# Sums, diagonals and spreads of norm factors in separate steps, and the order of the last scalings, in a one-core streaming-encoder block

## The chip, the cores and the metric

The kernel runs on 1 core of one Trainium2 chip. A core has five engines with queues of their own, which run side by side and meet at semaphores: TensorE (PE in the profile, with its weight loads as PEld), VectorE (DVE), ScalarE (ACT), GpSimd (POOL) and SyncE (SP), which here issues the DMAs. The metric is the device time of one execution in microseconds, the median of several.

## The reference, cut to what matters

One layer of a streaming encoder on 256 tokens of 2048 features, all float32:

```
x = x + 0.5 * swiglu(rms_norm(x, ffn1_norm), w_gate, w_up, w_down)
h = rms_norm(x, mix_norm);  proj = h @ w_in        # pool | q | k | v | g | a
y_pool = pool_mixer(u);  y_gla = gla_mixer(q, k, v, g, a)
x = x + concat(y_pool, y_gla) @ w_out
x = x + mem_cross_attention(rms_norm(x), rms_norm(mem))
x = x + 0.5 * swiglu(rms_norm(x, ffn2_norm), ...)
out = rms_norm(x, final_norm)
```

Two norms matter here. In `gla_mixer` each of 4 heads has 256 features per token, and after the attention of a head its output is normalised per token and head and then gated:

```
o = o * lax.rsqrt(jnp.mean(o * o, axis=-1, keepdims=True) + RMS_EPS)
o = o * head_norm;  return o * silu(g)
```

The other is the last `rms_norm`, over the 2048 features of each token, the end of the kernel.

## The kernel before, in words

**Precision and weights.** Each weight matrix is streamed once from memory in units of 1 MB (`raw`, three buffers). ACT casts a unit to its rounded half (`wh`, line 210), DVE subtracts to get the rest (`wl`, line 211); both have three buffers, so the cast of unit u+3 waits until TensorE has let go of unit u. Every product is made of several matmuls with these halves: in `block_a`, whose output has features on the partitions (lines 239 to 269), a unit is 32 matmuls (line 261) into two accumulators `pa`; in `block_b` (tokens on the partitions) and `block_t` a unit is 48 matmuls (line 276).

**The stream.** `Stream` (lines 34 to 77) records weight units and side steps. `st.op(f, n)` places step `f` behind the n-th unit from where it is recorded; all engines' work is issued from that one list. Then the framework's scheduler reorders within each engine's queue by its own estimates, so a queue's order is that of the built program and not only of the list. Each engine executes its queue strictly in order, and an instruction that waits holds all behind it.

**PSUM.** All matmul results go to one pool of four buffers (`ptile`, line 104), two of which a `block_a` holds during its units.

**The GLA part** (lines 670 to 763). `block_b` for the values `v` runs twice (b = 0, 1), with four units each. For the two heads of each b, `scores(h)` builds scaled queries `QD` on DVE (line 693), makes four products into `pq` (line 701) and copies them to `ST` (line 707); `attend(h)` makes the head's output `po` from `ST` and `v` (lines 714, 717), squares it on ACT into `osq` (line 723, tile `t`) and copies it to `oz` (line 725, tile `m`). `head_norms(b)` then handles the two heads of b at once, in one step:

1. `token_sums` (line 187): DVE adds the two halves of the squares (line 189), and TensorE sums over the partitions by a product with a column of ones (line 191, tile `pn`).
2. `rsqrt` (line 175): DVE and ACT compute the four factor columns `r` (lines 178 to 185; the square root on ACT).
3. `spread` (line 195): DVE makes a diagonal matrix from each factor column (line 198, two buffers), and TensorE spreads it over all partitions by a product with ones (line 199, tile `ps`).
4. DVE multiplies `oz` by the result (line 739).

After both b there are two `block_a` for the output gate g, four units each, whose evictions `ev_g` (lines 741 to 753) join the two halves of `pa` (ACT copies one half at line 234, DVE adds at line 235) and use the scaled `oz`. `head_norms(0)` and `scores`/`attend` of heads 2 and 3 thus stand between the units of the first gate block, and `head_norms(1)` between the two gate blocks.

`finish_norm` (line 222) does the same spreading for the norms before `w_in` and before `w_q`: the spread rows `R` are copied out at line 230.

**The end** (`down_end`, lines 900 to 979). The last product w_down is ordered so that the 128 tokens of the first half (h = 0) get their last unit for all four column blocks (nb 0 to 3) first, and then the second half (h = 1). Each finished block is added to X by DVE (line 934), squared with a row sum by ACT (line 937), and multiplied with the gain by POOL (line 939; not the very last block). `row_factor` (line 941) makes the row factor of a half, and `finish` (line 945) scales a block, on ACT (line 953) where it is told so or else on DVE (line 955; line 949 for the very last one), and sends it out (line 956). `second_half` (line 958) orders these: factor and four scalings of half 0, around the last products of half 1, then factor and scalings of half 1.

Of the kernel before, what the change touches and what calls it, by code (L numbers as in the profile page):

```python
# [7 lines left out]
F32 = mybir.dt.float32  # L8
F32R = mybir.dt.float32r
AF = mybir.ActivationFunctionType  # L10
ALU = mybir.AluOpType
# [3 lines left out]
P = 128  # L15
D = 2048
S = 256
# [62 lines left out]
def build(ctx, tc, I, out):  # L80
    nc = tc.nc
    st = Stream()
# [21 lines left out]
    def ptile(name):  # L104
        return psum.tile([P, 2, NB], F32, tag="ps", name=name)
# [6 lines left out]
    def uid(s):  # L112
        cnt[0] += 1
        return f"{s}{cnt[0]}"
# [60 lines left out]
    def rsqrt(dst, sums, n, w):  # L175

        v, r = chain[:, 0, :w], chain[:, 1, :w]
        nc.vector.tensor_scalar(
            out=v, in0=sums, scalar1=0.25 / n, scalar2=0.25 * EPS, op0=ALU.mult, op1=ALU.add
        )  # L180
        nc.scalar.activation(r, v, AF.Sqrt)
        nc.vector.reciprocal(out=dst, in_=r)
        nc.vector.tensor_tensor(out=v, in0=v, in1=dst, op=ALU.mult)
        nc.vector.tensor_tensor(out=v, in0=v, in1=r, op=ALU.add)
        nc.vector.reciprocal(out=dst, in_=v)

    def token_sums(out, sq):

        nc.vector.tensor_tensor(out=sq[:, 0, :], in0=sq[:, 0, :], in1=sq[:, 1, :], op=ALU.add)
        for t in range(2):  # L190
            nc.tensor.matmul(
                out[:, t : t + 1], sq[:, 0, t * P : (t + 1) * P], ones[:, 0:1], start=True, stop=True
            )

    def spread(ps, col, t):

        d = tmp.tile([P, P], F32, tag="diag", name=uid("diag"), bufs=2)
        nc.vector.tensor_scalar_mul(d, ident, col)
        nc.tensor.matmul(ps[:, t * P : (t + 1) * P], ones, d, start=True, stop=True)  # L199

    def split_scaled(dst, kt, src, scale):
# [14 lines left out]
    def row_squares(src, c):  # L216

        for h in range(2):
            j = tmp.tile([P, S], F32, tag="j", name=uid("j"), bufs=2)
            nc.scalar.activation(j, src[h], AF.Square, accum_out=ss[:, h, c : c + 1])  # L220

    def finish_norm(n, spread_too=True):

        nc.vector.tensor_reduce(out=sums, in_=ss[:, :, :n], axis=AX.X, op=ALU.add)
        rsqrt(Rcol, sums, D, 2)
        if spread_too:
            ps = ptile(uid("ps"))
            for t in range(2):
                spread(ps[:, 0, :], Rcol[:, t : t + 1], t)
            nc.vector.tensor_copy(R, ps[:, 0, :S])  # L230

    def joined(ps, dst, scale=None):
        c = ctile()
# [94 lines left out]
    def wblock(w, n0, k0=0, nk=KT):  # L328

        def src(k):  # L330
            return lambda raw: wload(raw.rearrange("p (k n) -> p k n", n=NB), w, k, 4, n0)
        return [src(k0 + k) for k in range(0, nk, 4)]
# [107 lines left out]
    def into_x(w, act, scale, gain=None, k0=0, nk=KT, spread_too=True):  # L440

        for b in range(2):
            block_t(wwide(w, b * 2 * NB, k0, nk), act, residual(scale, b))
            if gain is not None:
                for j in range(2):
                    st.op(lambda c=2 * b + j: fold(c, gain), 1)
        if gain is not None:
            st.op(lambda: finish_norm(4, spread_too), 2)

    FF_PARTS = ((0, 4), (4, 4), (8, 3))  # L450

# [58 lines left out]
    mix = {}  # L510
# [198 lines left out]
    def attend(h):  # L709
        s, v = mix["ST"], mix["v"]  # L710
        po = ptile(uid("po"))
        for vt in range(2):
            col = h * DV + vt * P
            nc.tensor.matmul(
                po[:, vt, :S], v[:, 0, col : col + P], s[:, 0, :], start=True, stop=False
            )
            nc.tensor.matmul(
                po[:, vt, 2 * CH : S], v[:, 1, col : col + P], s[:, 1, 2 * CH :], start=False, stop=True
            )
        if h % 2 == 0:  # L720
            mix["oz", h // 2] = as_four(m4())
        q = mix["osq", h] = ttile()
        nc.scalar.activation(q, po[:, :, :S], AF.Square)
        i = h % 2
        nc.vector.tensor_copy(mix["oz", h // 2][:, 2 * i : 2 * i + 2, :], po[:, :, :S])

    def head_norms(b):
        pn = ptile(uid("pn"))
        for i in range(2):
            token_sums(pn[:, 0, 2 * i : 2 * i + 2], mix["osq", 2 * b + i])  # L730
        r = mt("r", [P, 4])
        rsqrt(r, pn[:, 0, :4], DV, 4)
        ps = ptile(uid("ps"))
        for i in range(2):
            for t in range(2):
                spread(ps[:, i, :], r[:, 2 * i + t : 2 * i + t + 1], t)
        for i in range(2):
            oz = mix["oz", b][:, 2 * i : 2 * i + 2, :]
            nc.vector.tensor_tensor(out=oz, in0=oz, in1=bc(ps[:, i, :S]), op=ALU.mult)
# [15 lines left out]
    for b in range(2):  # L755
        block_b(wblock(w_in, (4 + b) * NB), xs, ev_v(b))
        for i in range(2):
            h = 2 * b + i
            st.op(lambda h=h: scores(h), 1 + i)
            st.op(lambda h=h: attend(h), 2 + i)  # L760
        st.op(lambda b=b: head_norms(b), 4)
    block_a(wblock(w_in, 6 * NB), xs, ev_g(0))
    block_a(wblock(w_in, 7 * NB), xs, ev_g(1))
    st.op(close_scope, 1)
# [135 lines left out]
    def down_end(wd, k0, nk):  # L900

        acc_ps, kept = {}, []

        def mm(b, k, h, wh, wl):

            wh, wl = (w.rearrange("p (k j n) -> p k j n", j=2, n=NB) for w in (wh, wl))
            for j in range(2):
                nb = 2 * b + j
                if nb not in acc_ps:
                    acc_ps[nb] = ptile(uid("pe"))  # L910
                for kk in range(2):
                    products(acc_ps[nb][:, h, :], ys, k + kk, h, wh[:, kk, j], wl[:, kk, j],
                             k + kk == 0, k + kk == nk - 1)
                if k == nk - 2:
                    end_evict(nb, h)

        def unit(b, k):
            def fn(wh, wl):
                for h in range(2):
                    mm(b, k, h, wh, wl)  # L920
            return fn

        def end_unit(b):
            def fn(wh, wl):
                kept.append((wh, wl))
                mm(b, nk - 2, 0, wh, wl)
            return fn

        def end_evict(nb, h):
            cols = slice(nb * NB, (nb + 1) * NB)  # L930
            if h == 0:
                fin[nb] = scope["pool"].tile([P, 2, NB], F32, tag="sg", name=uid("O"), bufs=4)
            xn, o = X[:, h, cols], fin[nb][:, h, :]
            nc.vector.scalar_tensor_tensor(
                out=xn, in0=acc_ps[nb][:, h, :], scalar=0.5, in1=xn, op0=ALU.mult, op1=ALU.add
            )
            nc.scalar.activation(o, xn, AF.Square, accum_out=ss[:, h, nb : nb + 1])
            if nb < 3 or h == 0:
                nc.gpsimd.tensor_tensor(out=o, in0=xn, in1=fin["gB"][:, cols], op=ALU.mult)

        def row_factor(h):
            nc.vector.tensor_reduce(out=sums[:, h : h + 1], in_=ss[:, h, :4], axis=AX.X, op=ALU.add)
            rsqrt(Rcol[:, h : h + 1], sums[:, h : h + 1], D, 1)

        def finish(h, c, engine=None):
            cols = slice(c * NB, (c + 1) * NB)
            x, o, r = fin[c][:, h, :], X[:, h, cols], Rcol[:, h : h + 1]
            if h == 1 and c == 3:
                nc.vector.scalar_tensor_tensor(
                    out=o, in0=o, scalar=r, in1=fin["gB"][:, cols], op0=ALU.mult, op1=ALU.mult  # L950
                )
            elif engine is nc.scalar:
                nc.scalar.activation(o, x, AF.Copy, scale=r)
            else:
                nc.vector.tensor_scalar_mul(o, x, r)
            nc.sync.dma_start(out[0, h * P : (h + 1) * P, cols], o)

        def second_half():
            row_factor(0)
            finish(0, 0, nc.scalar)  # L960
            finish(0, 3)
            for b in range(2):
                mm(b, nk - 2, 1, *kept[b])
            finish(0, 1)
            finish(0, 2)
            row_factor(1)
            for c in range(4):
                finish(1, c, nc.scalar if c == 1 else None)

        def ready_sqrt():  # L970
            tc.keep_in_program_order(nc.scalar.activation(sums, Rcol, AF.Sqrt))

        st.op(ready_sqrt, 8)
        for b in range(2):
            for i, src in enumerate(wwide(wd, b * 2 * NB, k0, nk - 2)):
                st.unit(src, unit(b, 2 * i))
        for b in range(2):
            st.unit(wwide(wd, b * 2 * NB, k0 + nk - 2, 2)[0], end_unit(b))
        st.op(second_half)
# [66 lines left out]
```

## Time and profile before

| | |
|---|---|
| median of 3 runs | 2189.62 us (2189.52 to 2190.53) |
| the profiled execution, whole | 2187.98 us |
| its span in the trace | 2186.0 us |
| TensorE busy | 2152.8 us, 98% of the span |
| VectorE, ScalarE, GpSimd busy | 1116.3, 918.3, 14.3 us |
| mean DMA rate | 185 GB/s |

The span is what the trace covers, the first to the last instruction or transfer; the whole execution is 1.98 us longer. "Busy" of an engine says nothing about whether it sets the end; for that the trace can be asked what an engine waited for, and when. A row of the timeline gives the start and the duration in microseconds, the engine, the line of the kernel, the operation, the tile written and the tiles read, the shape and how many instructions (or records) are in the row; in square brackets stands how long the engine was idle before and who released it. "PEclk" is TensorE's granted clock as a share of full speed.

### The profile page before, as it was taken

How to read it: one execution, taken by the hardware profiler on the slowest of the kernel's cores; microseconds unless marked ns; L12 is line 12 of the kernel's file. 1: busy time of each engine (PE TensorE's matmuls, PEld its weight loads, DVE VectorE, ACT ScalarE, POOL GpSimd, SP SyncE). 2: the span in 40 equal slices, each digit the busy share in tenths (PEclk: the TensorE clock that was granted, in tenths of full speed). 3: DMA queues.
4: the chain of work that ended last, by engine and by line, in shares of the span. 5: the costliest groups of instructions: out<-in, count | busy, mean ns of one | idle time of the engine just before them, and what ended most of it. 6: DMA issues, size and time to landing. Idle time of an engine off the chain costs nothing.

```text
span 2186.0 us, 23828 instructions
## 1 busy us (share of the span) xinstructions
PE 2152.8 (98%) x10194; PEld 1803.2 (82%) x10194; DVE 1116.3 (51%) x850; ACT 918.3 (42%) x811; POOL 14.3 (1%) x41
## 2 busy tenths in 40 slices
PE   9999999999999999889999999999999999999997
PEld 7888888888888888778888888888888888888886
DVE  5544444455455576555656554554554444444544
ACT  6333333333334554345445443444433334333333
POOL 0000000000000000000000000000000000000001
PEclk9999999999999999999999999999999999999999
DMA  7555555555555555446555455655555555555553
GB/s 274 194 189 192 193 188 190 194 182 193 194 187 193 174 176 175 134 140 224 175 192 173 155 171 177 191 184 194 181 193 192 192 193 192 185 195 195 195 176 114
DMA packets 134674, 404.45 MB, mean 185 GB/s; under 512 B 8868, under 2 KB 12040, under 8 KB 134184
## 3 DMA queue, kind: packets, MB, share of 16 engines
q1 hardware_dynamic: 134536, 402.92, 55.3%
q8 instruction: 80, 1.31, 0.2%
q14 instruction: 26, 0.21, 0.0%
q10 hardware_dynamic: 32, 0.01, 0.0%
HBM read 400.80 MB, written 2.10 MB: 184 GB/s over the span
## 4 chain that ended last, share of the span: by engine, by line
PE 98%; DVE 1%; ACT 0%; issue 0%; DMA 0%; SPq 0%; DVEq 0%; ACTq 0%
PE pt L276 71%; PE pa L261 15%; PE pb L276 6%; PE pe L276 3%; PE ph L473 1%; PE pl L831 1%; PE pv L866 1%; PE px L428 0%; ACT wh L210 0%; PE ps L199 0%; DMA X<-in_x 0%; PE px L394 0%; PE pa L592 0%; PE tm L793 0%; PE pq L701 0%
## 5 line engine op out<-in xcount | busy, mean ns | idle before, releaser
L211 DVE TENSOR_TENSOR wl<-raw,wh 128x2048 fp32r<-128x2048 f32 (+2 forms) x382 | 865.0, 2264 | 976.1 <-ACT wh L210 976.0
L210 ACT CAST wh<-raw 128x2048 fp32r<-128x2048 f32 (+2 forms) x383 | 722.0, 1885 | 1093.6 <-PE pt L276 887.3
L276 PE MATMUL pt<-wh,xs 128*128 128x512 f32 x2816 | 871.8, 390 | 0.0
L276 PEld LDWEIGHTS pt<-wh,xs 128*128 128x128 f32 x2816 | 528.9, 188 | 109.4
L276 PE MATMUL pt<-wl,xs 128*128 128x512 f32 x1408 | 548.2, 389 | 0.0
L276 PE MATMUL pt<-wh,ys 128*128 128x512 f32 x1728 | 535.1, 389 | 0.0
L276 PEld LDWEIGHTS pt<-wh,ys 128*128 128x128 f32 x1728 | 324.4, 188 | 67.0
L276 PE MATMUL pt<-wl,ys 128*128 128x512 f32 x864 | 336.3, 389 | 0.0
L261 PE MATMUL pa<-xs,wh 128*128 128x512 f32 x896 | 321.2, 402 | 0.0
L276 PEld LDWEIGHTS pt<-wl,xs 128*128 128x128 f32 x1408 | 264.6, 188 | 54.7
L261 PE MATMUL pa<-xs,wl 128*128 128x256 f32 x896 | 250.0, 282 | 0.0
L261 PEld LDWEIGHTS pa<-xs,wh 128*128 128x128 f32 x896 | 169.4, 190 | 40.2 <-issue 0.5
L276 PEld LDWEIGHTS pt<-wl,ys 128*128 128x128 f32 x864 | 162.2, 188 | 33.5
L261 PEld LDWEIGHTS pa<-xs,wl 128*128 128x128 f32 x896 | 170.6, 190 | 1.3
L276 PE MATMUL pb<-wh,xs 128*128 128x512 f32 x384 | 121.9, 392 | 0.5 <-DVE ys L203 0.5
L276 PEld LDWEIGHTS pb<-wh,xs 128*128 128x128 f32 x384 | 72.0, 188 | 15.8 <-DVE ys L203 0.7
L276 PE MATMUL pb<-wl,xs 128*128 128x512 f32 x192 | 74.9, 390 | 0.0
L276 PE MATMUL pe<-wh,ys 128*128 128x512 f32 x192 | 59.4, 390 | 0.0
L276 PEld LDWEIGHTS pe<-wh,ys 128*128 128x128 f32 x192 | 36.0, 188 | 7.5
L276 PEld LDWEIGHTS pb<-wl,xs 128*128 128x128 f32 x192 | 36.1, 188 | 7.2
L276 PE MATMUL pe<-wl,ys 128*128 128x512 f32 x96 | 37.5, 390 | 0.0
L458 ACT ACTIVATE sg<-pt,Rcol 128x512 f32<-128x512 f32 x44 | 27.9, 686 | 21.6 <-PE pt L276 21.5
(164 smaller groups left out, 694.7 us busy)
## 6 DMA issues: line engine op xcount, KB each, us to landing
raw<-in_ffn_w_down SPq DMA_DIRECT2D x88, 1024.0 KB, 5.1
raw<-in_ffn_w_up SPq DMA_DIRECT2D x80, 1024.0 KB, 4.9
raw<-in_ffn_w_gate SPq DMA_DIRECT2D x77, 1024.0 KB, 5.0
raw<-in_w_in SPq DMA_DIRECT2D x32, 1024.0 KB, 5.1
raw<-in_xattn_w_kv SPq DMA_DIRECT2D x32, 1024.0 KB, 5.2
raw<-in_w_out SPq DMA_DIRECT2D x16, 1024.0 KB, 5.3
raw<-in_xattn_w_q SPq DMA_DIRECT2D x16, 1024.0 KB, 5.0
raw<-in_xattn_w_o SPq DMA_DIRECT2D x16, 1024.0 KB, 5.2
```

The lines of the kernel that those rows point to most:

```text
L210: nc.scalar.copy(hi, src)
L211: nc.vector.tensor_tensor(out=lo, in0=src, in1=f32(hi), op=ALU.subtract)
L261: nc.tensor.matmul(o, w, x, start=k == 0 and i == 0, stop=last and i == 1)
L276: nc.tensor.matmul(ps, a, w, start=first and i == 0, stop=last and i == 2)
L458: nc.scalar.activation(g[:, h, :], ps[:, h, :], AF.Silu, scale=Rcol[:, h : h + 1])
L473: nc.tensor.transpose(v[:, i, h * P : (h + 1) * P], g[:, h, i * P : (i + 1) * P], ident)
L831: nc.tensor.matmul(ps[:, t, :M], ys[:, 4 * h + d, a, tok], xa["K"][:, d, b, :], start=i == 0, stop=i == 11,)
L866: nc.tensor.matmul(ps[:, d, :S], xa["V"][:, m, a, col], xa["PT"][:, m, b, :], start=i == 0, stop=i == 5,)
```

## The change

`head_norms` loses its first and last parts. The DVE additions of the squares become `head_squares(h)`, a step of its own behind `attend(h)`. `head_norms(b)` keeps the sums over the partitions and the factors, and now makes all four diagonals at once (four buffers in place of two). The spreading products and the scaling of `oz` become `head_scale(b)`, one unit later. In the same way `finish_norm` keeps the factors and the diagonals, and `spread_norm` has the spreading products and the copy to `R`; `finish_norm` is placed one unit earlier than before and `spread_norm` where the whole was. In `rsqrt` the two small DVE operations become one with two scalar operands where there is a single column, which is so in `row_factor` alone. In `second_half` the scaling of block 1 of half 0 moves from DVE to ACT, and it and that of block 2 are recorded between the last products of column blocks 0, 1 and those of 2, 3.

```diff
         nc.scalar.activation(r, v, AF.Sqrt)
         nc.vector.reciprocal(out=dst, in_=r)
-        nc.vector.tensor_tensor(out=v, in0=v, in1=dst, op=ALU.mult)
-        nc.vector.tensor_tensor(out=v, in0=v, in1=r, op=ALU.add)
+        if w == 1:
+            nc.vector.tensor_scalar(
+                out=v, in0=v, scalar1=dst, scalar2=r, op0=ALU.mult, op1=ALU.add
+            )
+        else:
+            nc.vector.tensor_tensor(out=v, in0=v, in1=dst, op=ALU.mult)
+            nc.vector.tensor_tensor(out=v, in0=v, in1=r, op=ALU.add)
         nc.vector.reciprocal(out=dst, in_=v)
 
-    def token_sums(out, sq):
-
-        nc.vector.tensor_tensor(out=sq[:, 0, :], in0=sq[:, 0, :], in1=sq[:, 1, :], op=ALU.add)
-        for t in range(2):
-            nc.tensor.matmul(
-                out[:, t : t + 1], sq[:, 0, t * P : (t + 1) * P], ones[:, 0:1], start=True, stop=True
-            )
-
-    def spread(ps, col, t):
-
-        d = tmp.tile([P, P], F32, tag="diag", name=uid("diag"), bufs=2)
+    def diagonal(col):
+        d = tmp.tile([P, P], F32, tag="diag", name=uid("diag"), bufs=4)
         nc.vector.tensor_scalar_mul(d, ident, col)
+        return d
+
+    def spread(ps, t, d):
+
         nc.tensor.matmul(ps[:, t * P : (t + 1) * P], ones, d, start=True, stop=True)
...
         if spread_too:
-            ps = ptile(uid("ps"))
-            for t in range(2):
-                spread(ps[:, 0, :], Rcol[:, t : t + 1], t)
-            nc.vector.tensor_copy(R, ps[:, 0, :S])
+            diag["R"] = [diagonal(Rcol[:, t : t + 1]) for t in range(2)]
+
+    def spread_norm():
+
+        ps = ptile(uid("ps"))
+        for t in range(2):
+            spread(ps[:, 0, :], t, diag["R"][t])
+        nc.vector.tensor_copy(R, ps[:, 0, :S])
...
         if gain is not None:
-            st.op(lambda: finish_norm(4, spread_too), 2)
+            st.op(lambda: finish_norm(4, spread_too), 1)
+            if spread_too:
+                st.op(spread_norm, 2)
...
+    def head_squares(h):
+        sq = mix["osq", h]
+        nc.vector.tensor_tensor(out=sq[:, 0, :], in0=sq[:, 0, :], in1=sq[:, 1, :], op=ALU.add)
+
     def head_norms(b):
         pn = ptile(uid("pn"))
         for i in range(2):
-            token_sums(pn[:, 0, 2 * i : 2 * i + 2], mix["osq", 2 * b + i])
+            sq = mix["osq", 2 * b + i]
+            for t in range(2):
+                nc.tensor.matmul(
+                    pn[:, 0, 2 * i + t : 2 * i + t + 1], sq[:, 0, t * P : (t + 1) * P],
+                    ones[:, 0:1], start=True, stop=True,
+                )
         r = mt("r", [P, 4])
         rsqrt(r, pn[:, 0, :4], DV, 4)
+        mix["diag"] = [diagonal(r[:, i : i + 1]) for i in range(4)]
+
+    def head_scale(b):
         ps = ptile(uid("ps"))
-        for i in range(2):
-            for t in range(2):
-                spread(ps[:, i, :], r[:, 2 * i + t : 2 * i + t + 1], t)
+        for i in range(4):
+            spread(ps[:, i // 2, :], i % 2, mix["diag"][i])
         for i in range(2):
             oz = mix["oz", b][:, 2 * i : 2 * i + 2, :]
             nc.vector.tensor_tensor(out=oz, in0=oz, in1=bc(ps[:, i, :S]), op=ALU.mult)
...
             st.op(lambda h=h: attend(h), 2 + i)
+            st.op(lambda h=h: head_squares(h), 2 + i)
         st.op(lambda b=b: head_norms(b), 4)
+        st.op(lambda b=b: head_scale(b), 5)
...
             finish(0, 3)
-            for b in range(2):
-                mm(b, nk - 2, 1, *kept[b])
-            finish(0, 1)
+            mm(0, nk - 2, 1, *kept[0])
+            finish(0, 1, nc.scalar)
             finish(0, 2)
+            mm(1, nk - 2, 1, *kept[1])
             row_factor(1)
```

In the built program TensorE's queue differs only between the second values block and the second gate block. There the partition sums of head 1 stand 48 gate matmuls later than before, all four spreads of b = 0 stand together behind 85 gate matmuls (before, the first one stood ahead of the block and the others within it), the scores of head 3 stand directly ahead of its attention (before, 20 gate matmuls lay between), and of b = 1 the sums of head 3 stand behind 27 matmuls of the second gate block and the four spreads behind 59. DVE's queue differs there and at the end, ACT's too; SP's and POOL's are the same but for which engine's result an output transfer waits on.

More of the change, by code (lines that the diff above doesn't have):

```diff
@@ L220, in row_squares @@
             nc.scalar.activation(j, src[h], AF.Square, accum_out=ss[:, h, c : c + 1])
+    diag = {}
     def finish_norm(n, spread_too=True):
```

## The prediction

> **What bounds the kernel now.** I read the page first, then TensorE's waits, then the timeline around each wait, with the granted clock over the same stretches, and last the end of the kernel.
>
> ```profile
> PE 2152.8 (98%) x10194; PEld 1803.2 (82%) x10194; DVE 1116.3 (51%) x850; ACT 918.3 (42%) x811; POOL 14.3 (1%) x41
> ...
> PE pn L191 <- DVE t L189: 9.7, 2, 4.9
> PE ps L199 <- DVE diag L198: 6.3, 2, 4.7
> ```
>
> TensorE is the bound, busy for 98% of the span. So a change elsewhere pays only where TensorE stands still, or behind its last matmul. The two rows from its waits (wait, total us, times, longest) are such places: 16.0 us in four waits, for exactly the steps that the diff takes apart. Where they lie:
>
> ```profile
> 894.10 0.38 PE L717 MATMUL po<-ST,v 128*128 128x128 f32 x2
> ...
> 898.78 0.41 DVE L189 TENSOR_TENSOR t<-t 128x256 f32<-128x256 f32 x1
> 899.34 0.98 PE L191 MATMUL pn<-ones,t 128*128 128x1 f32 x4 [4.86 <-DVE t L189]
> 900.36 0.16 DVE L178 TENSOR_SCALAR chain<-pn 128x4 f32<-128x4 f32 x1 [1.17 <-PE pn L191]
> ...
> 901.61 0.48 DVE L198 TENSOR_SCALAR diag<-ident,r 128x128 f32<-128x128 f32 x2
> 901.95 0.79 PE L199 MATMUL ps<-diag,ones 128*128 128x128 f32 x2 [1.63 <-DVE diag L198]
> 902.40 0.77 PE L261 MATMUL pa<-xs,wh 128*128 128x512 f32 x1
> ...
> 906.80 0.38 PE L199 MATMUL ps<-diag,ones 128*128 128x128 f32 x2
> ...
> 932.28 0.50 PE L191 MATMUL pn<-ones,t 128*128 128x1 f32 x4
> ...
> 937.67 0.98 PE L191 MATMUL pn<-ones,t 128*128 128x1 f32 x4 [4.89 <-DVE t L189]
> ...
> 943.33 0.77 PE L199 MATMUL ps<-diag,ones 128*128 128x128 f32 x2 [4.67 <-DVE diag L198]
> ...
> 947.98 0.38 PE L199 MATMUL ps<-diag,ones 128*128 128x128 f32 x2
> ```
>
> In each spot TensorE finishes an attention product, wants the partition sums at once and waits for ACT and DVE to square and add; then it wants the first spread and waits for the whole factor chain. Ready gate matmuls stand behind in its queue. And the loss goes on when it works again:
>
> ```profile
> 899.30:905.50 6.20, 4.53 (x15) 4.03 (x16) 1.61 (x8) 0.20 (x1) 0.00 (x0) 0.50 0.52 167
> ...
> 937.60:946.30 8.70, 3.95 (x14) 3.54 (x15) 4.84 (x15) 3.25 (x5) 0.00 (x0) 0.50 0.26 104
> ```
>
> In these stretches (busy time of PE, PEld, DVE, ACT, POOL, then the granted clock) the clock is 0.50 of full, right after the idle time.
>
> **What the two spots cost.** Full-speed prices come from the chain of waits:
>
> ```profile
> 747.62 9.89 PE pa L261 x56
> ...
> 879.43 0.43 PE po L714 x2
> 879.87 0.22 PE po L717 x2
> ...
> 906.96 0.22 PE ps L199 x2
> ```
>
> A gate matmul takes 9.89 / 56 = 0.177 us; one spread 0.22. The sums of one head take 0.50 (the row at 932.28; 0.98 at half clock). From the end of the attention (894.10 + 0.38 = 894.48) to the second spread (906.80) the work is sums, one spread and 16 gate matmuls: 0.50 + 0.22 + 16 x 0.177 = 3.55 us. It took 12.32, so spot 1 loses 8.77. In spot 2, from 932.78 to 947.98, the same work took 15.20: it loses 11.65. Together 20.4 us, 16.0 of it idle and the rest at the low clock.
>
> **What the new order does there.** I count matmuls in the built queue.
>
> Spot 1: the sums of head 1 now stand behind 48 gate matmuls, at 894.48 + 48 x 0.177 = 903.0; the added squares were ready at 898.78 + 0.41 = 899.2 already. The spreads stand behind 85, at 894.48 + 0.50 + 15.0 = 910.0. Their diagonals take longer than before, because the cast and subtraction of a weight unit now stand ahead of the square root. The prices are these:
>
> ```profile
> 896.34 1.28 ACT L181 ACT_TABLE_LOAD   x1
> ...
> 931.17 1.90 ACT L210 CAST wh<-raw 128x2048 fp32r<-128x2048 f32 x1
> ...
> 933.11 2.29 DVE L211 TENSOR_TENSOR wl<-raw,wh 128x2048 fp32r<-128x2048 f32 x1 [1.31 <-ACT wh L210]
> ...
> 935.32 0.68 DVE L237 TENSOR_TENSOR t<-t,R 128x512 f32<-128x512 f32 x1
> ```
>
> That cast waits for the buffer of the first gate unit, let go after 32 matmuls at 900.1, then 1.90 to 902.0 with the subtraction behind it to 904.3; the table load hides under it. From the chain's first operation to the end of two diagonals took 902.09 - 900.36 = 1.73 us; with two more, 2.2, so the diagonals are ready at 906.6, 3.4 us ahead of the spreads. Spot 1 goes to nothing, and the low clock with it.
>
> Spot 2 has new waits. Let T be the end of the first gate block. The queue then has the scores of head 3, its attention with nothing between, the sums of head 2, and the second gate block. The scores' prices:
>
> ```profile
> 889.82 0.38 PE L701 MATMUL pq<-m,k 128*64 128x128 f32 x2
> ...
> 890.43 1.37 DVE L707 COPY ST<-pq 64x256 f32<-64x256 f32 x4
> ```
>
> Scores take 0.80 and end there at 890.20; the four copies begin 0.23 later and take 1.37. Before, 20 gate matmuls (3.5 us) covered them. Now the attention waits: its first product (0.43) for two copies, some 1.04 us, its second for all four, until 1.70 behind the scores, another 0.23. That is 1.27 us of idle time. The attention and the sums then end at T + 0.80 + 2.57 + 0.50 = T + 3.87.
>
> The second wait is for PSUM. At that point all four buffers are taken: two by the first gate block's accumulators, one by the attention, one by the sums. The second gate block's first accumulator needs the first one's buffer, which ACT's copy and DVE's joining addition free; and that addition stands on DVE behind the copies of the scores (to T + 2.42) and one weight subtraction (2.29): it ends at T + 2.42 + 2.29 + 0.68 = T + 5.4. Idle time 1.58 us with the wake-up. That block's second accumulator waits for the next addition, 0.6 us on, hidden under 21 matmuls (3.7 us). The sums of head 3, behind 27 matmuls, are at T + 10.2, their squares ready at about T + 7; the spreads, behind 59, at T + 16.4, and their diagonals at about T + 13.5. No further wait.
>
> GLA part: 20.4 - 1.27 - 1.58 = 17.6 us saved. Bounds: both new waits absent, 20.4; both double, 14.7. Head 3's scores are nearly late too (16 matmuls or 2.8 us behind the attention of head 2, for square, copy, addition and six small scalings of about 2.9): at most 0.3, inside these bounds.
>
> **The other moves.** The spreads of the norms before w_in and w_q stand in the built queues where they stood, so they cost and bring nothing; had they moved earlier, DVE's diagonals would be the next to be late, and no TensorE wait names them today. Apart from one scaling that goes from DVE to ACT no engine gets more to do, no DMA is added, and SP's queue keeps its order.
>
> **The end.**
>
> ```profile
> 2169.35 5.07 POOL L939 TENSOR_TENSOR O<-X,gB 128x512 f32<-128x512 f32 x4 [0.35 <-ACT O L937]
> ...
> 2171.61 0.69 DVE L934 SCALAR_TENSOR_TENSOR X<-pe,X 128x512 f32<-128x512 f32 x1 [0.42 <-PE pe L276]
> ...
> 2172.22 0.15 DVE L182 RECIPROCAL Rcol<-chain 128x1 f32<-128x1 f32 x1
> ...
> 2172.34 0.63 ACT L937 ACTIVATE O<-X 128x512 f32<-128x512 f32 x1 [0.54 <-DVE X L934]
> 2172.41 0.76 DVE L183 TENSOR_TENSOR chain<-chain,Rcol 128x1 f32<-128x1 f32 x1
> ...
> 2173.20 1.24 DVE L184 TENSOR_TENSOR chain<-chain 128x1 f32<-128x1 f32 x1
> ...
> 2173.90 0.39 PE L276 MATMUL pe<-wh,ys 128*128 128x512 f32 x1
> 2174.36 0.68 DVE L934 SCALAR_TENSOR_TENSOR X<-pe,X 128x512 f32<-128x512 f32 x1
> ...
> 2175.21 2.29 DVE L955 TENSOR_SCALAR X<-O,Rcol 128x512 f32<-128x512 f32 x3
> ...
> 2175.70 0.70 ACT L953 ACTIVATE X<-O,Rcol 128x512 f32<-128x512 f32 x1
> ...
> 2175.87 1.34 POOL L939 TENSOR_TENSOR O<-X,gB 128x512 f32<-128x512 f32 x1 [1.45 <-ACT O L937]
> ...
> 2177.42 0.68 DVE L934 SCALAR_TENSOR_TENSOR X<-pe,X 128x512 f32<-128x512 f32 x1
> ...
> L955 DVE TENSOR_SCALAR X<-O,Rcol x5: 480/485/1491, 2175.2 to 2180.8; 128x512 f32<-128x512 f32 x5
> ```
>
> TensorE is done at 2174.29, but the last residual addition starts only at 2177.42: DVE is late. Two one-column operations took 0.76 and 1.24 us instead of 0.16; they end where POOL's multiplications end (5.07 / 4 = 1.27 each: 2173.15 and 2174.42). The third scaling took 1.49 instead of 0.48 and ended 0.29 behind POOL's at 2177.21. So DVE and POOL exclude each other there.
>
> The change replaces the two small operations by one with a single tensor operand; the similar one-column operation at line 178 ran in 0.15 to 0.16, so I take 0.16: the factor is there at 2172.75. The next addition waits for its product, 2174.29 - 6 matmuls of 0.227 = 2172.93, and ends at 2173.6. DVE still has two scalings ahead of the last addition: the first waits for POOL until 2174.42 and ends at 2174.71, the second at 2175.19. The last addition starts 2177.42 - 2175.19 = 2.23 us earlier. ACT's two scalings (0.70 each) run from 2173.1 to 2174.5, between squares, and it is free for the last square. The factor of the other half has one small operation less, 0.2. End: 2.4 us. Bounds: 3.3 if no scaling waits for POOL (the last addition then starts at about 2174.5); 0 if what ACT takes over delays its squares by the two scalings (1.4) and POOL then blocks DVE once more (1.0).
>
> Sum: 17.6 + 2.4 = 20.0. The profiled span goes to 2166.0; the whole profiled execution, 2187.98, was 1.64 below the median of the runs. Against that median: 2189.62 - 20.0 = 2169.6.
>
> **Rivals.**
>
> *The clock falls again.* Spot 2 still has some 2.9 us of idle time within 5.4 us. If the clock falls, the cost is that of one spot's low-clock part: 16 gate matmuls from 902.40 to 906.80 took 4.40 for 2.83, with sums and spread slowed by 0.9, 2.5 in all: 2172.1. For it: the falls at 0.50 above. Against: the idle times ahead of those were 4.86 and 4.89, three times the new ones. The Trainium skill, "TensorE: Matmul & The Clock Gate", "What's actually happening", puts the fall behind a whole idle window of about 3.4 us; by that, 1.3 and 1.6 would not do it. The trace agrees as far as it goes. Chance 0.13.
>
> *No new waits*, if the buffers come free sooner than I count: 2166.7. Against it is the queue order. 0.10.
>
> *The end gives nothing*: 2172.0. POOL takes its next block before DVE's second scaling, and the scaling moves behind it. I have POOL starting at 2175.3 and that scaling at 2174.7, a thin margin. The Trainium skill, "SBUF — State Buffer", "Who interferes with whom", says that whichever starts first holds the shared ports for its whole instruction, which speaks for this rival; the 1.49 us scaling agrees. 0.10.
>
> *The change doesn't do what it says*: in TensorE's queue nothing stands between the last products, and two scalings remain ahead of DVE's last addition. That is in my sum already; if spot 1 too stayed as it was (a factor chain 3.4 us later than I count), 2178.4. 0.02.
>
> *Slower*: the clock falls in spot 2 and stays low. At half clock a gate matmul takes 4.40 / 16 = 0.275, 0.098 more; over the 256 of both gate blocks 25 us, so 2194.7. It decides from 204 slow matmuls on (20.0 / 0.098). Against it: both times the trace shows full clock again within some 10 us. 0.03.
>
> **How the numbers follow.** The forecast has 0.62, with 2168.2 to 2171.3 as its own range (half of each new wait, half the end's gain). The range 2166.5 to 2173.5 adds the first three rivals and leaves out 0.12 or so. About 0.2% is what a measurement here can tell; all cases but the last are far below: faster 0.96, same 0.01, slower 0.03.
>
> **What would show it.** In the new profile TensorE's waits at the sums and spreads are gone; new ones stand at head 3's attention (about 1.3) and the next gate accumulator (about 1.6), with the clock at 1.00 throughout; the fused operation takes 0.16; the first of two DVE scalings about 1.0; and the last addition starts about 0.9 us behind TensorE's end. TensorE waits above 5 us in the GLA part, or a clock of 0.50 there, would make the prediction wrong.

## The result, and the profile after

| | before | after |
|---|---|---|
| median of 4 runs | 2189.57 us (2188.34 to 2190.53) | 2168.62 us (2167.38 to 2169.03) |
| ratio, with its 95% interval | | 0.9904 [0.9887, 0.9921] |
| the profiled execution, whole | 2187.98 us | 2167.38 us |
| its span | 2186.0 us | 2165.3 us |
| from the last matmul's end to the end of the span | 11.76 us | 9.29 us |

The change makes the kernel faster by 20.95 us (0.96%), where 20.0 were forecast. In what follows lines of the changed kernel have other numbers: the gate matmuls stand at L267, the partition sums at L744, the attention at L722 and L725, the last additions at L955, the scalings at L974 (ACT) and L976 (DVE).

TensorE's waits in the changed kernel (who waited, for whom, total us, times, longest):

```profile
PE pgain L381 <- DMA gain<-in_ffn_norm: 4.1, 1, 4.1
PE pa L267 <- DVE t L241: 1.7, 1, 1.7
PE po L722 <- DVE ST L715: 1.0, 1, 1.0
PE pp L573 <- DVE k L241: 0.6, 1, 0.6
```

The two rows of 9.7 and 6.3 us are gone. In their place are the two waits that the prediction found in the queue: head 3's attention waits for the copies of its scores, and the second gate block's first accumulator waits for a joining addition (L241 is the one at line 235 before).

The best yardstick for the GLA part is one stretch that does the same matmuls in every version: from the first matmul of head 1's attention to the first of the product with w_out. Two views by windows, the kernel before and the changed one (window, its length, busy time of PE, PEld, DVE, ACT, POOL with their instruction counts, the granted clock, DMA share, GB/s):

```profile
892.57:968.13 75.56, 59.51 (x330) 51.52 (x328) 36.14 (x60) 26.53 (x28) 0.00 (x0) 0.89 0.34 111
```

```profile
892.76:949.83 57.07, 54.38 (x329) 47.58 (x328) 36.12 (x60) 26.87 (x28) 0.00 (x0) 1.00 0.45 146
```

The stretch is 18.5 us shorter. TensorE's idle time in it went from 16.05 us (75.56 - 59.51) to 2.69 (57.07 - 54.38), and its busy time fell by 5.13 for the same matmuls, because the clock stayed at 1.00. Behind the stretch nothing changed up to the last matmul: 2174.29 - 968.13 = 1206.16 us before, 2155.99 - 949.83 = 1206.16 after. So the divided norm before w_q, which lies there, brought nothing and cost nothing.

The places in the changed kernel's timeline:

```profile
902.84 0.50 PE L744 MATMUL pn<-ones,t 128*128 128x1 f32 x4
...
905.54 0.87 DVE L194 TENSOR_SCALAR diag<-ident,r 128x128 f32<-128x128 f32 x4
...
909.88 1.05 PE L199 MATMUL ps<-diag,ones 128*128 128x128 f32 x8
...
921.52 1.38 DVE L715 COPY ST<-pq 64x256 f32<-64x256 f32 x4 [0.98 <-PE pq L709]
922.47 0.67 PE L722 MATMUL po<-ST,v 128*128 128x256 f32 x2 [1.03 <-DVE ST L715]
...
922.93 2.29 DVE L211 TENSOR_TENSOR wl<-raw,wh 128x2048 fp32r<-128x2048 f32 x1
...
925.25 1.29 DVE L241 TENSOR_TENSOR t<-pa,c 128x512 f32<-128x512 f32 x2
926.09 0.47 PE L267 MATMUL pa<-xs,wh 128*128 128x512 f32 x1 [1.65 <-DVE t L241]
```

The sums were forecast at 903.0, the diagonals ready at 906.6, the spreads at 910.0; they are at 902.84, 906.41 and 909.88, without a wait. The second new wait is read from the last three rows: DVE does a whole weight subtraction of 2.29 us, then the addition that frees the buffer, and only then does the gate matmul start.

And the end:

```profile
2154.10 0.27 DVE L184 TENSOR_SCALAR chain<-chain,Rcol 128x1 f32<-128x1 f32 x1
...
2154.66 0.69 DVE L955 SCALAR_TENSOR_TENSOR X<-pe,X 128x512 f32<-128x512 f32 x1
2154.67 1.34 ACT L974 ACTIVATE X<-O,Rcol 128x512 f32<-128x512 f32 x2
...
2155.27 1.53 DVE L976 TENSOR_SCALAR X<-O,Rcol 128x512 f32<-128x512 f32 x2
...
2155.60 0.39 PE L282 MATMUL pe<-wh,ys 128*128 128x512 f32 x1
...
2156.73 0.68 DVE L955 SCALAR_TENSOR_TENSOR X<-pe,X 128x512 f32<-128x512 f32 x1
```

The fused operation takes 0.27 us where two took 0.76 and 1.24. The last addition starts 0.74 us behind TensorE's end (2155.60 + 0.39 = 2155.99), where it was 3.13.

### The profile page after: what moved, and what is told of

Read it like the earlier page. It is cut to its first block, busy times and chain, and to the rows that moved or that the text cites. A ratio compares the mean times of both kernels' runs of the same rounds, so it can differ in the third digit from the quotient of the medians.

```text
span 2165.3 us, 23828 instructions
## 1 busy us (share of the span) xinstructions
PE 2147.6 (99%) x10194; PEld 1798.8 (83%) x10194; DVE 1114.0 (51%) x847; ACT 919.2 (42%) x812; POOL 14.2 (1%) x41
## 4 chain that ended last, share of the span: by engine, by line
PE 99%; DVE 1%; DMA 0%; issue 0%; ACT 0%; SPq 0%; DVEq 0%; ACTq 0%
PE pt L282 71%; PE pa L267 15%; PE pb L282 6%; PE pe L282 3%; PE ph L481 1%; PE pl L852 1%; PE pv L887 1%; PE px L434 0%; DMA X<-in_x 0%; PE px L400 0%; PE pa L600 0%; PE tm L814 0%; PE pq L709 0%; PE po L722 0%; PE ps L199 0%
## 5 line engine op out<-in xcount | busy, mean ns | idle before, releaser
L267 PE MATMUL pa<-xs,wh 128*128 128x512 f32 x896 | 317.6, 398 | 1.7 <-DVE t L241 1.7
L267 PE MATMUL pa<-xs,wl 128*128 128x256 f32 x896 | 248.9, 281 | 0.0
L267 PEld LDWEIGHTS pa<-xs,wh 128*128 128x128 f32 x896 | 167.8, 188 | 41.0 <-issue 2.0
L267 PEld LDWEIGHTS pa<-xs,wl 128*128 128x128 f32 x896 | 169.2, 189 | 1.5 <-issue 0.2
```

What stands on the lines that cost most here:

```text
L267: nc.tensor.matmul(o, w, x, start=k == 0 and i == 0, stop=last and i == 1)
```

## The experiments

All times are medians; where a run is compared with the kernel before, that was run on the same chip. Beside the ratio each entry gives what separates the two parts of the change: the stretch of the GLA part as above, and the end, from the last matmul to the end of the span.

### The GLA part alone, and the end alone

The changed kernel with the end of the kernel before:

```diff
-        if w == 1:
-            nc.vector.tensor_scalar(out=v, in0=v, scalar1=dst, scalar2=r, op0=ALU.mult, op1=ALU.add)
-        else:
...
-            mm(0, nk - 2, 1, *kept[0])
-            finish(0, 1, nc.scalar)
+            for b in range(2):
+                mm(b, nk - 2, 1, *kept[b])
+            finish(0, 1)
             finish(0, 2)
-            mm(1, nk - 2, 1, *kept[1])
```

> The change without its two edits at the end of the kernel (two small operations and the old order of the scalings as before). If the gain is made of a GLA part and an end that add up, TensorE's last matmul ends where it does with the whole change (18.3 us sooner than before) and what follows it lasts 11.7 us as before, in place of 9.3: some 2171.0 us. If the two depend on each other (the end gains only because DMA or the clock are in another state by then), what follows the last matmul is not 11.7 and the time is below 2170 or above 2173.

Measured: 2170.96 us, ratio 0.9916 [0.9901, 0.9931]; stretch 57.07, end 11.76.

The kernel before with those same two edits at the end:

```diff
-            for b in range(2):
-                mm(b, nk - 2, 1, *kept[b])
-            finish(0, 1)
+            mm(0, nk - 2, 1, *kept[0])
+            finish(0, 1, nc.scalar)
             finish(0, 2)
+            mm(1, nk - 2, 1, *kept[1])
```

and the one-column operation of the change in `rsqrt`.

> The kernel before with the two edits at the end alone. If the parts add up: TensorE's last matmul as before, 9.3 us behind it in place of 11.7, so about 2187.2 us, with all four waits of 16.0 us in the GLA part still there and the granted clock at 0.50 behind them. If the end's gain needs the GLA part, about 2189.6.

Measured: 2186.91 us, ratio 0.9991 [0.9981, 1.0]; stretch 76.4, end 9.28. The ratio alone hardly tells 2 us from nothing; the end in the trace does: 9.28 in place of 11.76, as in the changed kernel, with TensorE's waits of 9.8 and 6.3 us still there. So the two parts are independent: 18.5 and 2.5 us, together 21.0.

### Which of the three divisions mattered

The kernel before, with the additions of the squares as a step of their own and nothing else:

```diff
     def token_sums(out, sq):
-        nc.vector.tensor_tensor(out=sq[:, 0, :], in0=sq[:, 0, :], in1=sq[:, 1, :], op=ALU.add)
...
+    def head_squares(h):
+        sq = mix["osq", h]
+        nc.vector.tensor_tensor(out=sq[:, 0, :], in0=sq[:, 0, :], in1=sq[:, 1, :], op=ALU.add)
...
             st.op(lambda h=h: attend(h), 2 + i)
+            st.op(lambda h=h: head_squares(h), 2 + i)
```

> The kernel before with one thing changed: the additions of the squares are a step of their own behind each attention; partition sums, factors, diagonals and spreads stay one step in their old place. If the late additions are what TensorE waited for (the row of 9.7 us names them), the two waits of 4.9 us at the sums shrink and 5 to 10 us are saved: 2180 to 2185. If the place of the whole step among the gate units is the cause, and the addition is only the last thing before the sums, nothing changes: 2189.6, waits of 9.7 and 6.3 us as before.

Measured: 2188.77 us, ratio 1.0001 [0.9991, 1.001]. Its TensorE waits:

```profile
PE pn L190 <- DVE t L728: 9.7, 2, 4.9
PE ps L198 <- DVE diag L197: 6.3, 2, 4.7
```

The row still names the addition, now at its new line, and the wait is the same to a tenth. In this run the addition for which TensorE waits did not come any earlier: it starts 4.30 us behind head 1's attention, as before, since DVE first does a weight subtraction and the copy of the attention's output (rows under "Place, or PSUM buffers"). So the run shows that this division alone does nothing, and not what an earlier addition would do. But in the changed kernel the addition starts just as late, 4.29 us behind the attention (898.98 - 894.69), and nobody waits for it. What a wait names is what came last, and that need not be what to move.

The changed GLA part with the additions back inside the step of the sums, and the old end:

```diff
-            st.op(lambda h=h: head_squares(h), 2 + i)
...
         for i in range(2):
+            head_squares(2 * b + i)
             sq = mix["osq", 2 * b + i]
```

> The kernel before with the other thing changed: the spreads and the scaling are a step of their own one unit later, with four diagonals; the additions of the squares stay with the sums, in their old place. The end is as before. If the additions mattered, the waits of 9.7 us at the sums stay, and the clock falls: 2180 to 2185. If moving the spreads is enough, it equals the GLA part alone, some 2171.0, with waits of 1.0 and 1.7 us as with the whole change.

Measured: 2169.92 us, ratio 0.9914 [0.9897, 0.993]; stretch 57.2, end 11.77, waits of 1.7 and 1.0. It is the GLA part alone. The division of the additions is worth nothing; putting the spreads off by one unit is worth all.

### Division, or place

The kernel before with one number changed, and nothing divided:

```diff
-        st.op(lambda b=b: head_norms(b), 4)
+        st.op(lambda b=b: head_norms(b), 5)
```

> The kernel before with one number changed: the undivided step of sums, factors, diagonals and spreads stands one unit later (5 in place of 4). If the place behind the gate block's first unit is what the change bought, the four waits of 16.0 us go without taking anything apart, only a wait of about 1.3 us at head 3's attention stays, and the time is 2169 to 2171 with the old end. If the division is needed (the undivided step must wait for its own factors wherever it stands), waits at the spreads of 1.6 and 4.7 us stay and the time is 2178 or more.

Measured: 2168.88 us, ratio 0.9908 [0.9894, 0.9923], with the old end (11.8 us). The only TensorE wait in the GLA part:

```profile
PE po L714 <- DVE ST L707: 1.0, 1, 1.0
```

So division isn't needed at all. The step one unit later, whole, gives the gain of the GLA part, and without the wait of 1.7 us. In its built queue 47 gate matmuls stand ahead of head 1's sums, and the spreads come later still.

### Place, or PSUM buffers

The kernel before, step undivided and in its old place, but it takes one of the four PSUM buffers in place of two:

```diff
-        pn = ptile(uid("pn"))
+        ps = ptile(uid("ps"))
+        pn = ps[:, 1, S:]
         for i in range(2):
-            token_sums(pn[:, 0, 2 * i : 2 * i + 2], mix["osq", 2 * b + i])
+            token_sums(pn[:, 2 * i : 2 * i + 2], mix["osq", 2 * b + i])
         r = mt("r", [P, 4])
-        rsqrt(r, pn[:, 0, :4], DV, 4)
-        ps = ptile(uid("ps"))
+        rsqrt(r, pn[:, :4], DV, 4)
```

> The kernel before with the step undivided and in its old place, but the sums go into a free corner of the PSUM buffer that the spreads use, so that the step takes one buffer of four in place of two. If it was the lack of a PSUM buffer that kept the gate block's second accumulator, and with it the gate matmuls, behind the factors, all four waits go although every step is where it was: 2168 to 2170 with the old end, clock at 1.00. If the place in the list is the cause, nothing changes: 2189.

Measured: 2168.08 us, ratio 0.9904 [0.9888, 0.9921], with the old end. The stretch in the view by windows:

```profile
892.93:948.06 55.13, 55.13 (x329) 47.51 (x328) 35.85 (x60) 26.76 (x28) 0.00 (x0) 1.00 0.46 152
```

TensorE is busy for all 55.13 us; no wait is left, the clock is 1.00. In the built program of the kernel before, the spreads' tile takes the one buffer that is free when the gate block begins; the gate block's two accumulators get that of the values, and that of head 1's attention, which DVE empties with the copy just ahead of the addition at 898.78, 4 us after the attention's last matmul:

```profile
895.85 2.29 DVE L211 TENSOR_TENSOR wl<-raw,wh 128x2048 fp32r<-128x2048 f32 x1 [4.05 <-ACT wh L210]
898.17 0.69 DVE L725 COPY m<-po 128x512 f32<-128x512 f32 x1
```

With one buffer less in the step, the free one goes to the gate block. But the buffer is not all that differs. The list has every step where it was; the built queue has not. Before, the sums of head 1 and the first spread stood ahead of all gate matmuls. Here 46 gate matmuls stand ahead of those sums and 76 ahead of the first spreads, which in this trace are at

```profile
903.48 0.61 PE L191 MATMUL ps<-ones,t 128*128 128x1 f32 x4
...
911.31 0.61 PE L199 MATMUL ps<-diag,ones 128*128 128x128 f32 x4
```

So this run shows that one buffer less is enough, by way of another queue; it does not tell the buffer from the order.

The changed kernel with that buffer held from the start of the sums:

```diff
     def head_norms(b):
+        mix["ps"] = ptile(uid("ps"))
+        nc.tensor.matmul(mix["ps"][:, 1, S : S + P], ones, ident, start=True, stop=True)
         pn = ptile(uid("pn"))
...
     def head_scale(b):
-        ps = ptile(uid("ps"))
+        ps = mix["ps"]
```

> The whole change, but the spreads' PSUM buffer is taken from the beginning of the sums on, by a product of ones with the identity written into a corner of it that nobody reads (0.2 us of TensorE twice). The gate block's accumulators then get the same buffers as in the kernel before: the second one waits until head 1's attention is copied out. If the buffer alone made the waits of before, they come back (TensorE waits above 10 us in the GLA part, clock at 0.50, 2180 or more). If it took both, the buffer and the spreads standing ahead of the gate matmuls in the queue, the first accumulator's matmuls fill the time, and only the wait in front of the second gate block grows, by some 1 to 3 us: 2169 to 2173.

Measured: 2170.69 us in a single run. The wait ahead of the second gate block doubled, and the old waits didn't come back:

```profile
PE pa L267 <- DVE t L241: 3.4, 1, 3.4
```

So holding the buffer does not bring the old waits back. In this version's queue 45 matmuls of the first accumulator and two of the second stand ahead of head 1's sums, and they fill the time. What every version without the old waits has in common is that order: gate matmuls ahead of the awaited sums and spreads. A place one unit later brings it about, and so does one buffer less. That the old order would wait with a free buffer as well follows from a queue that is worked through strictly in order; no run here has that combination, so it is argued and not shown. How the scheduler comes from the buffers to its order is open too.

### The two waits that were left

The changed kernel with the spreads and the scaling of the heads one more unit later:

```diff
-        st.op(lambda b=b: head_scale(b), 5)
+        st.op(lambda b=b: head_scale(b), 6)
```

> The whole change with the spreading and scaling of the heads placed one more unit later (6 in place of 5). In the built queue the scores of head 2 then no longer stand behind the spreads, and 30 or so gate matmuls lie between each scores step and its attention. If the two waits left in the GLA part (1.0 and 1.7 us) come from head 3 being pushed together with its attention and from four PSUM buffers being taken at once, both go and 2.5 to 3 us are saved: some 2166.0 us, no TensorE wait in the GLA part. If they belong to the data (factors late at any place), they move and the time stays at 2168.6.

Measured: 2165.39 us (2165.0 to 2165.86), ratio 0.9892 [0.9877, 0.9907]. The stretch:

```profile
893.47:948.09 54.62, 54.62 (x329) 47.67 (x328) 36.00 (x60) 26.77 (x28) 0.00 (x0) 1.00 0.47 153
```

No wait is left in it. Between the scores of head 3 and its attention stand 11 gate matmuls again, not the 30 that I had named; these 1.9 us are enough for the copies.

The kernel before with one buffer (the diff of that experiment) and the two edits at the end comes to the same:

> The kernel before with the step undivided and in its old place, its sums in a corner of the spreads' PSUM buffer, and the two edits at the end. If GLA part and end add up here too, it is the kernel with one buffer (2168.1) less 2.4: 2165.7, equal within 0.5 to the version with the scaling one more unit later, so that dividing the steps buys nothing that one buffer less does not. If the division is worth something of its own, it stays 1 us or more above that version's 2165.4.

Measured: 2165.51 us (2165.3 to 2165.68), ratio 0.9892 [0.9875, 0.9908]; stretch 55.1, end 9.3. Both beat the kernel before by 1.08%. Their medians lie 3.1 to 3.2 us below that of the changed kernel, but these were measured apart, and the intervals of the ratios overlap. The traces account for 57.07 - 54.62 = 2.45 us in the first and 57.07 - 55.13 = 1.94 in the second; the rest is not explained.

### The end, in its two edits

The changed kernel with the old order of the scalings, the fused operation kept:

```diff
-            mm(0, nk - 2, 1, *kept[0])
-            finish(0, 1, nc.scalar)
+            for b in range(2):
+                mm(b, nk - 2, 1, *kept[b])
+            finish(0, 1)
             finish(0, 2)
-            mm(1, nk - 2, 1, *kept[1])
```

> The whole change with the old order of the last scalings: three of half 0 on DVE ahead of the last addition, one on ACT; the one-column operation stays fused. Read from TensorE's last matmul to the end of the span (11.7 us before, 9.3 with the whole change). If DVE and POOL exclude each other, the fused operation is free of POOL (0.27 us), the first scaling waits for POOL to 0.1 us behind TensorE's end, and the third scaling costs 0.5 to 1.8 more: 9.9 to 11.0. If the fused operation bought nothing, 11.7.

Measured: 2169.86 us in one run; end 10.70 us. Three scalings stand ahead of the last addition again:

```profile
2155.16 0.27 DVE L184 TENSOR_SCALAR chain<-chain,Rcol 128x1 f32<-128x1 f32 x1
...
2156.33 2.93 DVE L976 TENSOR_SCALAR X<-O,Rcol 128x512 f32<-128x512 f32 x3
...
2159.18 0.68 DVE L955 SCALAR_TENSOR_TENSOR X<-pe,X 128x512 f32<-128x512 f32 x1
```

The changed kernel with the two small operations again, the new order kept:

```diff
-        if w == 1:
-            nc.vector.tensor_scalar(out=v, in0=v, scalar1=dst, scalar2=r, op0=ALU.mult, op1=ALU.add)
-        else:
-            nc.vector.tensor_tensor(out=v, in0=v, in1=dst, op=ALU.mult)
-            nc.vector.tensor_tensor(out=v, in0=v, in1=r, op=ALU.add)
+        nc.vector.tensor_tensor(out=v, in0=v, in1=dst, op=ALU.mult)
+        nc.vector.tensor_tensor(out=v, in0=v, in1=r, op=ALU.add)
```

> The whole change with the two small one-column operations in place of the fused one; the scalings as in the change. The two operations read two tensors each and run beside POOL: if the exclusion holds, they take 0.7 and 1.2 us again, the factor comes 1.9 us later, and ACT's two scalings, which stand ahead of its last squares, hold those back: some 11.0 us from TensorE's last matmul to the end. If their slowness before was chance, they take 0.16 each and the end lasts 9.3 to 9.5.

Measured: 2170.92 us in one run; end 10.54 us. The small operations are slow again, beside POOL:

```profile
2153.26 5.08 POOL L955 TENSOR_TENSOR O<-X,gB 128x512 f32<-128x512 f32 x4 [0.35 <-ACT O L953]
...
2156.32 0.75 DVE L183 TENSOR_TENSOR chain<-chain,Rcol 128x1 f32<-128x1 f32 x1
...
2157.11 1.25 DVE L184 TENSOR_TENSOR chain<-chain 128x1 f32<-128x1 f32 x1
```

They end at 2157.07 and 2158.36, where POOL's third and fourth multiplications end (2153.26 + 3 and 4 times 1.27: 2157.07 and 2158.34). So each edit alone brings about half: 11.76 - 10.70 = 1.06 for the fused operation, 11.76 - 10.54 = 1.22 for the order, 2.5 for both. My expectation that ACT's scalings would hold back its squares hardly came true: in the built queue the square of block 2 stands ahead of them there, and only the last square starts some 0.2 us later for them.

## Why the prediction was right, point by point

- *TensorE bounds, and only its waits and the end pay.* Right. The two parts add up (18.5 and 2.5, each run alone).
- *The loss of the two spots, 20.4.* A little small. In the stretch of 75.56 us the kernel before lost 75.56 - 54.38 = 21.2 us: 16.05 idle and 5.13 by the low clock. I had 4.4 for the clock, in part since I priced the sums of each spot at full speed with 0.50 from their row; in the changed kernel's chain of waits they take 0.34. With the smaller new waits this makes the GLA part 18.5 where 17.6 were forecast.
- *The new waits, 1.27 and 1.58.* Right in place and cause; they took 1.03 and 1.65. TensorE's idle time in the stretch is 2.69 against 2.85. Removing the crowding (the version with the scaling one more unit later) removed both.
- *The cause of the old waits.* The prediction named TensorE's order ("wants the partition sums at once") and counted on the new order as built. That order is what all versions without the old waits have changed, so the mechanism held. What the prediction did not have is what brings the new order about: the late additions of the squares stayed as late, the division was not needed, and one PSUM buffer less in the step did as much as a later place.
- *The end, 2.4.* Right: 11.76 to 9.29, 2.5. The fused operation takes 0.27, not 0.16, and the two scalings 1.53, not 1.56 (2175.19 - 2173.63); the first waited for POOL, as forecast. Two small misses cancel, which is luck: the last addition starts 3.13 - 0.74 = 2.39 us sooner behind TensorE's end, not 2.23, and the factor of the other half gains 0.07, not 0.2 (from its first operation to the scalings 1.53 us before, 1.46 after).
- *The rivals.* "The end gives nothing" fell: POOL's next block started at 2156.70, when DVE's second scaling was nearly done. "No new waits" fell, though a one-digit edit makes it true. "The clock falls again" did not occur in the profiled execution of the changed kernel, yet it did in another version with the same two waits, for 1.5 us and not the 2.5 that I had named; see below.
- *The numbers around the forecast.* The upper end of the narrower range, 2171.3, does not follow from the terms that it names: half of the new waits gives 2169.6 + 1.43 = 2171.0, half of the end's gain 2170.8.

## What to carry to other kernels

Where a queue in strict order waits, ask not only who came last but why ready work stands behind the waiting instruction in the built queue; a step that takes one buffer fewer, or stands one unit later, can be worth as much as one cut in pieces. Before dividing a step, move it whole: here one number gave what the division gave. And beside POOL's multiplications, prefer for a single column the form of an operation with one tensor operand: 0.27 us here against 0.75 to 1.25. For whole blocks that form was not enough: the scaling of a 128x512 block has one tensor operand, and it waited for POOL all the same (1.49 us against 0.48).

## What the runs showed of the hardware that I had not expected

The granted clock can fall although TensorE never stands still for long. Five profiled executions have the same TensorE queue around the two new waits (the changed kernel, its GLA part alone, the version with the additions put back, and the two versions of the end), with the same waits of 1.0 and 1.7 us. In four of them the clock is 1.00 throughout. In the one with the two small operations it is not; its stretch of the GLA part, the wait itself, and the time right behind:

```profile
893.49:952.05 58.56, 55.87 (x329) 48.85 (x328) 36.02 (x60) 26.85 (x28) 0.00 (x0) 0.97 0.43 143
...
921.00:926.80 5.80, 3.13 (x23) 2.31 (x22) 4.67 (x9) 4.56 (x5) 0.00 (x0) 1.00 0.39 156
926.80:930.20 3.40, 3.38 (x15) 2.92 (x15) 3.30 (x7) 1.26 (x2) 0.00 (x0) 0.72 0.84 275
```

TensorE was busy for 3.13 of 5.80 us, at full clock. The clock fell only after work had begun again, 1.5 us later: from 928.3 to 931.7 it was 0.50. The stretch is 1.5 us longer than the 57.07 of the changed kernel. The clock fell in the version with the buffer held too (0.97 over its stretch), behind its one wait of 3.4 us. So 2.7 us of idle time in pieces within 6 us were followed by a loss of another 1.5 in one of five executions. The Trainium skill, "TensorE: Matmul & The Clock Gate", "What's actually happening", lets the clock fall after at least one idle window of about 3.4 us, a window that runs freely. The free running fits what differs between executions of one queue. If idle means that nothing runs in the window, the trace disagrees: no idle piece before this fall was longer than 1.7, and TensorE was busy for 1.75 of the last 3.41 us ahead of it.

The other is how sharply DVE and POOL exclude each other even at a single column: a DVE operation on one column with two tensor operands took 0.75 to 1.25 us beside POOL's 1.27 us multiplications, and 0.16 in the other half's factor, where POOL rests (the kernel before and the version with the two small operations), while one with a single tensor operand and two scalar columns took 0.27 in both places. The Trainium skill, "SBUF — State Buffer", "Who interferes with whom", says that a DVE instruction with two SBUF inputs contends with a GpSimd instruction that reads SBUF, and that one with at most one SBUF input does not, as long as it is outside the modes that use both ports. The traces agree for the single column. The block scalings, which have one tensor operand and waited, would then be in such a mode; no run here shows whether they were.
